# Transposes some steps later, banks' additions ahead of later remainders, and the norm's work in pieces: a two-layer hybrid encoder on one core

## The chip, the core and the metric

The kernel runs on one core of one Trainium2 chip. The metric is the device time of the core in microseconds, and the number compared is the median of several runs. The core has five engines that matter here. TensorE (PE; its weight loads are listed as PEld) multiplies. VectorE (DVE) and ScalarE (ACT) do elementwise work and read the accumulators. GpSimd (POOL) does elementwise work on the main on-chip memory and issues some transfers. SyncE (SP) issues most transfers. Each engine has its own queue of instructions and they meet only at semaphores.

## The reference

The reference is a trunk of two residual layers over 256 tokens of width 2048, in float32. Each layer adds a token mixer and then a gated feed-forward part, each of them on the RMS-normed tokens:

```
for i in range(DEPTH):                     # DEPTH = 2
    h = rms_norm(x, norm_mix[i])
    if i % 2 == 0:
        mix = attention_mixer(h, ...)      # 16 query heads, 4 key heads of 128, softmax over 256 tokens
    else:
        mix = recurrent_mixer(h, ...)      # two projections, conv of width 4, two gated scans, output projection
    x = x + mix
    x = x + swiglu(rms_norm(x, norm_ffn[i]), w_gate, w_up, w_down)   # width 5632
```

In the attention mixer, queries and keys of each head are RMS-normed and rotated before the scores. In the recurrent mixer, the x branch is convolved, goes through a forward and a backward gated linear recurrence, and is multiplied by GELU of the gate branch.

## The kernel before

**Numbers in two parts.** TensorE gets every float32 operand as two parts: a rounded part (`hi`) and a remainder (`lo`), and a product is three matmuls (hi·hi, hi·lo, lo·hi). Weights come in halves of 128 x 1024 numbers (512 KB). `load_half` loads one into `raw` (SP's queue), ScalarE casts it to `hi` (L129) and VectorE subtracts to get the remainder `lo` (L130). Each of the three tiles has 5 buffers. The list `order` holds all 704 halves in the order in which TensorE takes them, and `taken[0]` counts them.

**Who sets the order.** TensorE's order is that of the program text. The order of the other engines is laid by a planner that simulates the program and picks ready instructions by their place in it. Two things bind the planner: `follow(i, j)` puts instruction i behind j on its engine without a semaphore, and `in_line` chains the casts on ScalarE, and the remainders on VectorE, in the order of the halves. `in_line` is on only in the feed-forward parts, where `line` is filled (`line.update`) and afterwards cleared.

**A clock of steps.** `step()` counts half products of TensorE (three matmuls are two steps; in the three-matmul sums of the recurrent mixer one step). `later(delay, fn)` puts work off until the count has gone on by `delay`; one item comes at each step at most, in the order in which they were put in. So the attention's small matmuls are strewn among the projections' large ones: the keys' transposes (`KEY_TURN`, `turn_heads`, L663), the queries' (`TURN_Q`), the scores of the four heads of a group (`SCORES`, L719), the transposes of the softmax's probabilities (`TURN_P` after the scores, L737), and the sums of values (`VALUES`, L751). The keys' operand is `hq`, scaled by `scale` on VectorE (L677); the probabilities are scaled on GpSimd (L731) by the reciprocal of their sum (L729). `flush` runs what is left at the end of the attention.

**Accumulators.** The large products go into four banks of the pool `ps_a` (tag `acc`), the small ones into four of `ps_m` (tag `pm`). `project_tokens` fills two banks from 8 halves (`token_half`). `project_pair` fills four banks, for two column blocks j = 0, 1: some steps for both blocks, then the rest of block 0, then the rest of block 1. At a step in `forms` it does the two halves of a block pair in seven products instead of eight (`seven_forms`: L295 to L304 make the sums of weights that this needs; the second half comes through `sr`, which GpSimd's queue loads and adds up in flight). `merge` (L385 to L389) puts the seven products together. When block j is complete, `done(j, banks)` adds the banks to what they belong to on VectorE: gate (L819), up (L822), residual tokens `x_tok` (L565, L542). In the recurrent mixer L896 takes the gate branch's bank. Only then can the bank be filled anew.

**The norm.** `Norm.add(c)` is called when a column block of 512 of the residual is complete: squares on ScalarE, `turned` (two 32 x 32 block transposes on VectorE and 16 copies, eight of them on each of two engines, L516), and four operands (a cast, L462, and a subtraction, L463). It ran in one go. `owed` is a list of pieces of work that `project_pair` calls between halves with `settle`; before, only the transposes, copies and casts of a feed-forward unit's result (L836 to L850) go through it.

## Time and profile before

| | |
|---|---|
| median of 3 runs | 1980.67 us (1979.37 to 1981.26) |
| profiled execution | 1983.66 us |
| its span, first to last instruction | 1981.9 us |
| TensorE's mean granted clock | 0.998 |
| HBM traffic over the span | 216 GB/s |

One execution was profiled. Its time is that of the whole execution, its span that from the first to the last instruction. All stages and rows below are in microseconds from the start of the span. The profile's page gives the busy share of each engine; the list of waits says which engine waited for whom; the timeline gives start, length and, in brackets, the idle time before an instruction and what ended it. A matmul's length includes the time in the pipeline, so two matmuls in a row overlap in it. The stages of the time before lie so: keys and values from 6 to 50, queries with the attention in between from 50 to 170, the attention's output from 170 to 270, the feed-forward part of layer 0 from 270 to 968, the recurrent mixer from 968 to 1199, its output from 1199 to 1288, the feed-forward part of layer 1 from 1288 to the end.

### The profile page before, as it was taken

The page shows a single profiled execution, that of the slowest core. Times are in us where ns is not written, and L with a number is a line of the kernel's source. Part 1 is how long each engine was busy: PE and PEld are TensorE (multiplying, and loading weights), DVE is VectorE, ACT ScalarE, POOL GpSimd, SP SyncE. Part 2 cuts the span into 40 slices and gives each one's busy share as a digit, 9 for nine tenths or more (in the row PEclk, how much of TensorE's full clock was granted, in tenths as well). Part 3 has the DMA queues.
Part 4 walks back from the last instruction along what each step waited for, and adds up shares of the span by engine and source line. Part 5 has one row for each costly group of instructions (what it writes and reads, how often), then busy time and mean ns, then how long its engine had stood idle before and what let it go on. Part 6 is the DMA issues. An engine that isn't in the chain of part 4 may idle for free.

```text
span 1981.9 us, 27557 instructions
## 1 busy us (share of the span) xinstructions
PE 1962.5 (99%) x9665; PEld 1661.3 (84%) x9665; DVE 1686.6 (85%) x2273; ACT 1347.1 (68%) x2050; POOL 221.6 (11%) x317
## 2 busy tenths in 40 slices
PE   9999999999999999999999999999999999999999
PEld 7788887888888888888899998888888888888887
DVE  6676888867999988999978886998768999989998
ACT  6566667655677656677798986767746776567773
POOL 0011101000001110011033331000000101011010
PEclk9999999999999999999999999999999999999999
DMA  8544657767767876676656556567767778777784
GB/s 332 168 139 133 202 198 214 248 213 221 231 217 241 264 251 222 232 230 221 204 172 193 183 175 208 192 210 225 228 206 229 232 227 266 230 252 228 231 262 166
DMA packets 133771, 430.75 MB, mean 217 GB/s; under 512 B 14976, under 2 KB 15872, under 8 KB 133376
## 3 DMA queue, kind: packets, MB, share of 16 engines
q1 hardware_dynamic: 109008, 362.11, 53.2%
q0 software_dynamic: 24480, 66.86, 13.9%
q8 instruction: 76, 1.25, 0.3%
q14 instruction: 63, 0.52, 0.1%
q10 hardware_dynamic: 144, 0.02, 0.0%
HBM read 426.83 MB, written 2.10 MB: 216 GB/s over the span
## 4 chain that ended last, share of the span: by engine, by line
PE 83%; DVE 8%; issue 4%; ACT 4%; DMA 2%; POOL 0%; SPq 0%; DVEq 0%; ACTq 0%; POOLq 0%
PE acc L339 51%; PE acc L256 9%; PE pm L339 9%; PE acc L394 3%; PE acc L393 3%; PE acc L395 3%; DVE lo L130 3%; ACT tf L842 1%; PE pm L256 1%; ACT hi L129 1%; PE pm L394 1%; PE pm L393 1%; PE pm L395 1%; DMA raw<-in_w_gate_dram 1%; DVE lo L301 1%
## 5 line engine op out<-in xcount | busy, mean ns | idle before, releaser
L130 DVE TENSOR_TENSOR lo<-raw,hi 128x1024 fp32r<-128x1024 f32 (+1 forms) x620 | 748.9, 1225 | 168.2 <-ACT hi L129 163.6
L129 ACT CAST hi<-raw 128x1024 fp32r<-128x1024 f32 (+1 forms) x620 | 638.0, 1047 | 316.3 <-PE acc L339 171.1
L339 PE MATMUL acc<-hi,xg 128*128 128x512 f32 x1920 | 614.1, 389 | 3.3 <-DVE fg L819 3.1
L339 PE MATMUL acc<-hi,act 128*128 128x512 f32 x1370 | 434.1, 390 | 2.3 <-DVE x_tok L565 1.2
L339 PEld LDWEIGHTS acc<-hi,xg 128*128 128x128 f32 x1920 | 360.4, 188 | 79.9 <-DVE fg L819 4.0
L339 PE MATMUL acc<-lo,xg 128*128 128x512 f32 x960 | 373.5, 389 | 0.0
L339 PEld LDWEIGHTS acc<-hi,act 128*128 128x128 f32 x1370 | 257.2, 188 | 56.3 <-DVE x_tok L565 1.8
L339 PE MATMUL acc<-lo,act 128*128 128x512 f32 x685 | 266.7, 389 | 1.3 <-DVE lo L130 1.3
L339 PEld LDWEIGHTS acc<-lo,xg 128*128 128x128 f32 x960 | 180.2, 188 | 37.3
L842 ACT COPY tf<-tb 32x256 f32<-32x256 f32 x352 | 142.2, 404 | 17.3 <-DVE tb L836 13.4
L339 PEld LDWEIGHTS acc<-lo,act 128*128 128x128 f32 x685 | 128.7, 188 | 27.8 <-DVE lo L130 1.7
L394 PE MATMUL acc<-xg,hi 128*128 128x256 f32 x512 | 144.8, 283 | 0.6 <-DVE xg L463 0.6
L393 PE MATMUL acc<-xg,hi 128*128 128x256 f32 x512 | 144.9, 283 | 0.1
L395 PE MATMUL acc<-xg,lo 128*128 128x256 f32 x512 | 144.4, 282 | 0.0
L302 ACT CAST wxh<-raw 128x1024 fp32r<-128x1024 f32 x85 | 89.3, 1050 | 74.0 <-DVE raw L300 73.5
L281 POOL DMA_DIRECT2D sr<-in_w_up_dram x64 | 35.6, 557 | 775.1 <-DVE lo L301 694.0
L298 ACT CAST wxh<-wx 128x512 fp32r<-128x512 f32 x85 | 52.8, 621 | 91.6 <-DVE wx L295 58.8
L297 ACT CAST hi<-sr 128x1024 fp32r<-128x1024 f32 x85 | 89.3, 1051 | 35.2 <-PE acc L339 31.4
L304 DVE TENSOR_TENSOR wxl<-raw,wxh 128x1024 fp32r<-128x1024 f32 x85 | 103.5, 1217 | 7.6 <-ACT wxh L302 7.6
L256 PE MATMUL acc<-hi,xg 128*128 128x512 f32 x320 | 109.3, 402 | 0.4 <-ACT hi L129 0.4
L301 DVE TENSOR_TENSOR lo<-sr,hi 128x1024 fp32r<-128x1024 f32 x85 | 103.4, 1217 | 0.0
L394 PEld LDWEIGHTS acc<-xg,hi 128*128 128x128 f32 x512 | 97.9, 191 | 0.9 <-DVE xg L463 0.8
(212 smaller groups left out, 3178.4 us busy)
## 6 DMA issues: line engine op xcount, KB each, us to landing
raw<-in_w_gate_dram SPq DMA_DIRECT2D x176, 512.0 KB, 5.4
raw<-in_w_down_dram SPq DMA_DIRECT2D x155, 512.0 KB, 5.1
raw<-in_w_up_dram SPq DMA_DIRECT2D x112, 512.0 KB, 5.6
sr<-in_w_up_dram POOLq DMA_DIRECT2D x64, 512.0 KB, 4.7
raw<-in_w_in_dram SPq DMA_DIRECT2D x64, 512.0 KB, 4.5
raw<-in_w_qkv_dram SPq DMA_DIRECT2D x48, 512.0 KB, 4.3
raw<-in_w_o_dram SPq DMA_DIRECT2D x32, 512.0 KB, 3.5
wx<-in_w_up_dram SPq DMA_DIRECT2D x64, 256.0 KB, 4.6
```

The lines of the kernel that those rows point to most:

```text
L129: newest["cast"] = in_line("act", act.copy(hi[:, sl, :], raw[:, sl, :]))
L130: in_line("dve", dve.tensor_tensor(lo[:, sl, :], raw[:, sl, :], hi[:, sl, :].bitcast(F32), ALU.subtract))
L256: pe.matmul(accs[a], x, wt[:, k, :], start=(k0 + k == 0 and n == 0), stop=(end and k == 1 and n == 2))
L297: in_line("act", act.copy(hi, raw))
L301: in_line("dve", dve.tensor_tensor(lo, raw, hi[:].bitcast(F32), ALU.subtract))
L302: in_line("act", act.copy(xh[:, 1:, :], r1))
L304: in_line("dve", dve.tensor_tensor(xl[:, 1:, :], r1, xh[:, 1:, :].bitcast(F32), ALU.subtract))
L339: pe.matmul(acc, a, b, start=id(acc) not in begun, stop=last and i == 2)
L393: pe.matmul(o, hi, x[:, :S], start=start, stop=False)
L394: pe.matmul(o, hi, x[:, S:], start=False, stop=False)
L395: pe.matmul(o, lo, x[:, :S], start=False, stop=stop)
L842: n = act.copy(f[32 * i : 32 * i + 32, q::4, :, :], b[32 * q : 32 * q + 32, :, i, :, :])
```

## The change

- `KEY_TURN` goes from (36, 44) to (62, 68) steps. `TURN_P` becomes one number for each head, 16 for the first two and 20 for the others. The second entry of `VALUES` goes from 94 to 98.
- `not_after(i)` notes that instruction i has to come ahead of the remainder of the half `taken[0] + 3`; `settled`, called with each remainder, then makes this remainder follow i on VectorE. Bound like this are the additions L819, L822, L565, L542 and, for the last two column tiles, L896. `seven_forms` counts its two halves one by one for this.
- `Norm.add` no longer does its work at once but puts six pieces into `owed`: squares and block transposes, four pieces of four copies, and the operands. In the feed-forward parts the copies follow the newest cast and the newest remainder. The last column's call does all that is owed at once. `token_half` calls two pieces for each half, `project_pair` one, or two where more than six are owed; at a step for one block, all are called only where the step before was for both.
- The first weight half is loaded in two transfers and the second one is loaded and cast in two; x's tiles 2 and 3 are loaded behind the second half instead of the first.

The diff without the pure moves of `owed` and `settle`:

```diff
-KEY_TURN = (36, 44)
+KEY_TURN = (62, 68)
-TURN_P = 16
-VALUES = (62, 94)
+TURN_P = (16, 16, 20, 20)
+VALUES = (62, 98)
...
+    due = {}
+
+    def not_after(i, ahead=3):
+        due.setdefault(taken[0] + ahead, []).append(i)
+
+    def settled(i, n):
+        for k in [k for k in due if k <= n]:
+            for j in due.pop(k):
+                follow(i, j)
...
-        newest["load"] = sync.dma_start(out=raw[:, :n, :], in_=src[:, :n, :])
+        for i in range(pieces):
+            sl = slice(i * n // pieces, (i + 1) * n // pieces)
+            newest["load"] = sync.dma_start(out=raw[:, sl, :], in_=src[:, sl, :])
...
-            in_line("dve", dve.tensor_tensor(lo[:, sl, :], raw[:, sl, :], hi[:, sl, :].bitcast(F32), ALU.subtract))
+            rest = in_line("dve", dve.tensor_tensor(lo[:, sl, :], raw[:, sl, :], hi[:, sl, :].bitcast(F32), ALU.subtract))
+            settled(rest, taken[0] - 1)
...
             scale_x(0)
+            return load_half(*order[n], 2)
+        if n == 1:
             return load_half(*order[n], 2, partial(load_x, 2, 2))
...
     def token_half(accs, xs, k0):
         half()
+        settle(2)
...
-        taken[0] += 2
+        taken[0] += 1
         load_half(*order[i])
+        taken[0] += 1
...
-        in_line("dve", dve.tensor_tensor(lo, raw, hi[:].bitcast(F32), ALU.subtract))
+        settled(in_line("dve", dve.tensor_tensor(lo, raw, hi[:].bitcast(F32), ALU.subtract)), taken[0] - 1)
...
-            if len(cols) == 1:
+            if len(cols) == 1 and i and len(plan[i - 1][1]) == 2:
                 settle(-1)
                 if ready:
                     ready()
-                    ready = None
...
                 if i:
-                    settle()
+                    settle(2 if len(owed) > 6 else 1)
...
         def add(self, c):
-            for a in range(2):
-                act.activation(tmp("nj", (P, WIDE), mybir.dt.bfloat16, 1), x_tok[:, a, c, :], AF.Square, accum_out=self.sums[:, a, c : c + 1])
-            behind = self.finish() if c == NCOL - 1 else None
-            for f in turned(x_tok[:, :, c, :], True, behind):
-                self.operand(f, True)
...
+            last = c == NCOL - 1
+            parts = []
+            fields = {}
+
+            def first():
+                for a in range(2):
+                    act.activation(tmp("nj", (P, WIDE), mybir.dt.bfloat16, 1), x_tok[:, a, c, :], AF.Square, accum_out=self.sums[:, a, c : c + 1])
+                fields["behind"] = self.finish() if last else [line.get(e) for e in ("act", "dve")]
+                fields["b"] = fp[0].tile([P, 2, FOUR, P], F32, tag="tb", name=nm("tb"))
+                fields["f"] = fp[0].tile([P, 8, FOUR, 32], F32, tag="tf", name=nm("tf"))
+                for a in range(2):
+                    dve.transpose(fields["b"][:, a, :, :], x_tok[:, a, c, :])
+
+            def copies(q):
+                b, f = fields["b"], fields["f"]
+                behind = fields["behind"] if last else [line.get(e) for e in ("act", "dve")]
+                for i in range(4):
+                    o, y = f[32 * i : 32 * i + 32, q::4, :, :], b[32 * q : 32 * q + 32, :, i, :]
+                    n = (dve.tensor_copy if i % 2 else act.copy)(o, y.rearrange("p a (k t) -> p a k t", k=FOUR))
+                    if behind and behind[i % 2] is not None:
+                        follow(n, behind[i % 2])
+
+            def operands():
+                for k in range(FOUR):
+                    self.operand(fields["f"][:, :, k, :], True)
...
+            owed.extend([first, *(partial(copies, q) for q in range(4)), operands])
+            if last:
+                settle(-1)
...
-                dve.tensor_tensor(y, y, acc, ALU.add)
+                not_after(dve.tensor_tensor(y, y, acc, ALU.add))
...
-            later(TURN_P, turn)
+            later(TURN_P[h], turn)
...
-                        dve.tensor_tensor(g[:, a, :], acc, g[:, a, :], ALU.add)
+                        not_after(dve.tensor_tensor(g[:, a, :], acc, g[:, a, :], ALU.add))
...
-                        dve.tensor_tensor(u[:, a, :], acc, u[:, a, :], ALU.add)
+                        not_after(dve.tensor_tensor(u[:, a, :], acc, u[:, a, :], ALU.add))
...
-        dve.tensor_tensor(y, acc, nr.r, ALU.mult)
+        i = dve.tensor_tensor(y, acc, nr.r, ALU.mult)
+        if ct >= KT - 2:
+            not_after(i)
```

More of the change, by code (lines that the diff above doesn't have):

```diff
@@ L272, in square, with settle @@
         return t.rearrange("p c f -> p (c f)")
+    owed = []
+    def settle(n=1):
+        while owed and n:
+            owed.pop(0)()
+            n -= 1
     coming, ahead = [], []
@@ L319, in x_forms @@
         return [(t[:, 0, i, :], t[:, 1, i, :]) for i in range(4)]
-    owed = []
-    def settle(n=1):
-        while owed and n:
-            owed.pop(0)()
-            n -= 1
     def project_pair(xs, forms, plan, middle, done, ready=None):
@@ L468, in add @@
         def add(self, c):
-            for a in range(2):
-                act.activation(tmp("nj", (P, WIDE), mybir.dt.bfloat16, 1), x_tok[:, a, c, :], AF.Square, accum_out=self.sums[:, a, c : c + 1])
-            behind = self.finish() if c == NCOL - 1 else None
-            for f in turned(x_tok[:, :, c, :], True, behind):
-                self.operand(f, True)
-            for n in THREE[1:] if self.seven else ():
-                if FOUR * c <= 2 * n < FOUR * c + FOUR:
-                    self.forms[n] = x_forms(self.xs[2 * n], self.xs[2 * n + 1], f"nf{n}")
+            last = c == NCOL - 1
[20 more added lines that the diff above has]
+                    self.operand(fields["f"][:, :, k, :], True)
+                for n in THREE[1:] if self.seven else ():
+                    if FOUR * c <= 2 * n < FOUR * c + FOUR:
+                        self.forms[n] = x_forms(self.xs[2 * n], self.xs[2 * n + 1], f"nf{n}")
+            owed.extend([first, *(partial(copies, q) for q in range(4)), operands])
+            if last:
+                settle(-1)
         def finish(self):
@@ L502, in spread @@
             return i
-    def turned(src, both=True, behind=None):
-        b = fp[0].tile([P, 2, FOUR, P], F32, tag="tb", name=nm("tb"))
-        f = fp[0].tile([P, 8, FOUR, 32], F32, tag="tf", name=nm("tf"))
-        for a in range(2):
-            dve.transpose(b[:, a, :, :], src[:, a, :])
-        for q in range(4):
-            for i in range(4):
-                o, y = f[32 * i : 32 * i + 32, q::4, :, :], b[32 * q : 32 * q + 32, :, i, :]
-                y = y.rearrange("p a (k t) -> p a k t", k=FOUR)
-                turn = dve.tensor_copy if i % 2 and both else act.copy
-                n = turn(o, y)
-                if behind is not None:
-                    follow(n, behind[i % 2])
-        return [f[:, :, k, :] for k in range(FOUR)]
     fp = []
```

2 lines of the change are left out of this document (1 added, 1 removed).

## The prediction

> **What bounds the kernel now.** I read the page first, then the list of waits, then the timeline of each engine around every place where TensorE stood still. The share of busy time comes from the page, the other lines from the list of waits (engine, line, whom it waited for: us in total, times, longest):
> ```profile
> PE 1962.5 (99%) x9665; PEld 1661.3 (84%) x9665; DVE 1686.6 (85%) x2273; ACT 1347.1 (68%) x2050; POOL 221.6 (11%) x317
> ```
> ```profile
> PE acc L339 <- DVE fg L819: 3.1, 2, 2.4
> ...
> PE pm L663 <- DVE hq L677: 3.0, 1, 3.0
> ...
> PE pm L737 <- POOL pr L731: 1.9, 3, 0.6
> ...
> PE acc L339 <- DVE lo L130: 1.3, 1, 1.3
> PE acc L339 <- DVE x_tok L565: 1.2, 1, 1.2
> ...
> PE acc L339 <- DVE gl L896: 1.1, 1, 1.1
> ...
> PE pm L256 <- DVE lo L130: 0.8, 1, 0.8
> ```
> TensorE is the bound: 1962.5 of 1981.9 us. No edit here removes a matmul, so all that can be won are those waits and what hangs on them. They are few and each has one place. What else can matter is how far VectorE runs ahead, so here are stretches of the trace (busy us and count of PE, weight load, DVE, ACT, POOL, then the granted clock, DMA share, GB/s); the last is a whole unit of the feed-forward part:
> ```profile
> 60.00:64.00 4.00, 1.00 (x5) 0.54 (x3) 3.90 (x9) 0.70 (x2) 0.00 (x0) 0.89 0.56 155
> ...
> 66.00:68.00 2.00, 2.00 (x6) 1.61 (x5) 0.69 (x1) 0.06 (x1) 0.00 (x0) 0.50 0.01 4
> ...
> 823.70:865.50 41.80, 41.80 (x183) 34.23 (x183) 39.54 (x51) 30.22 (x44) 4.25 (x6) 1.00 0.75 239
> ```
> The unit gives 183 matmuls in 41.80 us: one starts every 0.228 us, though one takes 0.39. So an idle stretch costs its length, plus 0.39 - 0.23 = 0.16, plus 0.11 because the matmul behind it takes 0.50: **idle + 0.27 us**. And VectorE is busy 39.54 of 41.80 us there: it has next to no time to spare.
>
> **Part 1, keys' transposes (36, 44 to 62, 68 steps).**
> ```profile
> 60.45 0.39 PE L256 MATMUL acc<-hi,xg 128*128 128x512 f32 x1
> 63.84 1.50 PE L663 MATMUL pm<-ident,hq 128*128 128x128 f32 x4 [3.00 <-DVE hq L677]
> ...
> 70.14 0.60 PE L663 MATMUL pm<-ident,hq 128*128 128x128 f32 x4
> ...
> 63.10 1.29 DVE L677 TENSOR_TENSOR hq<-hq,hf 128x512 f32<-128x512 f32 x2
> ```
> From 60.45 to 70.14 are 9.69 us; in them lie 13 matmuls (2.96 at 0.228) and four transposes (0.4). The other 6.3 are lost: 3.2 of waiting, 0.9 of transposes that come one by one (1.50 for four instead of 0.60), and 2.3 because the clock row shows 0.50 afterwards. A step is half a product of three matmuls, 0.34 us, so 26 steps move the transposes 8.9 us back, to about 69.7; their operand is there at 64.4. The second pair moves 24 steps, behind the first. Nothing needs the keys before the first scores, which come at step 222 of the count against 188. The same eight transposes, four casts and subtractions remain, so only their place changes. I take **-6.3** (bounds: -3.9, if the slow clock struck for another reason, to -6.4).
> [...]
>
> **Part 2, probabilities' transposes of heads 2 and 3 (16 to 20 steps).**
> ```profile
> 117.37 1.00 PE L737 MATMUL pm<-ident,pr 128*128 128x128 f32 x4 [0.64 <-POOL pr L731]
> ...
> 116.83 0.93 POOL L731 TENSOR_SCALAR pr<-pr,rs 128x256 f32<-128x256 f32 x2 [5.51 <-DVE rs L729]
> ```
> Three groups have this wait, all at head 3, whose scores collide with the next group's squares and rotation: 1.9 idle in the list, and three times 0.16 + (1.00 - 0.60), 3.5 in all. Four steps are 1.36 us against 1.2 of lateness, so it just suffices. **-3.3** (-1.2 to -3.5). The weighted sum of values moves from 94 to 98 with it; in the last group the flush at step 96 catches it, 8 steps (2.7 us) ahead of its use, which covers one cast and one subtraction.
>
> **Part 3, banks' additions bound ahead of the remainder three halves later.** The order on VectorE is what is edited: no instruction is added.
> ```profile
> 314.14 1.22 DVE L301 TENSOR_TENSOR lo<-sr,hi 128x1024 fp32r<-128x1024 f32 x1
> ...
> 315.88 0.68 DVE L819 TENSOR_TENSOR fg<-acc,fg 128x512 f32<-128x512 f32 x1
> ...
> 316.61 0.50 PE L339 MATMUL acc<-hi,xg 128*128 128x512 f32 x1 [2.42 <-DVE fg L819]
> ...
> 1332.04 0.50 PE L339 MATMUL acc<-hi,xg 128*128 128x512 f32 x1 [0.70 <-DVE fg L819]
> ...
> 1376.77 0.50 PE L339 MATMUL acc<-hi,xg 128*128 128x512 f32 x1 [0.22 <-DVE fu L822]
> ...
> 1204.55 0.50 PE L339 MATMUL acc<-hi,act 128*128 128x512 f32 x1 [1.06 <-DVE gl L896]
> ...
> 924.01 0.50 PE L339 MATMUL acc<-hi,act 128*128 128x512 f32 x1 [1.22 <-DVE x_tok L565]
> ```
> A new unit needs the banks of the last; their additions stood behind remainders not needed for another 5 us (L301 ahead of L819). Bound, they run as soon as the bank is closed. At 316.61, 1332.04 and 1376.77 this frees 2.7 + 1.0 + 0.5 = 4.2 us. But VectorE's work is not less, and its remainders for the next units come no sooner:
> ```profile
> 333.08 2.35 DVE L130 TENSOR_TENSOR lo<-raw,hi 128x1024 fp32r<-128x1024 f32 x2
> ...
> 336.01 0.39 PE L339 MATMUL acc<-lo,xg 128*128 128x512 f32 x1
> ...
> 375.74 2.35 DVE L130 TENSOR_TENSOR lo<-raw,hi 128x1024 fp32r<-128x1024 f32 x2
> ...
> 377.80 0.39 PE L339 MATMUL acc<-lo,xg 128*128 128x512 f32 x1
> ...
> 330.98 0.69 DVE L303 TENSOR_TENSOR wxl<-wx,wxh 128x512 fp32r<-128x512 f32 x1 [3.05 <-ACT wxh L298]
> ```
> The remainder used at 336.01 is done at 333.08 + 1.2 = 334.3, 1.7 us ahead; one unit later (377.80) it is 0.9 ahead. If TensorE comes 2.7 us sooner and VectorE doesn't, the wait returns there and only 0.9 stays. VectorE's own 3.05 idle in between (it waits behind ScalarE's 16 copies, which start after the additions) can shrink, so up to all can stay. I take 1.1 and 0.9 for the two layers, **-2.0** (-0.9 to -4.2). At 1204.55 nothing of the kind follows (the list has a single wait of this stage's products on a remainder, that of part 4): **-1.3** (0 to -1.3). At 924.01 it is 1.5, counted in part 4.
> What the binding costs: where VectorE runs ahead it now waits for the bank.
> ```profile
> 499.68 1.28 DVE L819 TENSOR_TENSOR fg<-acc,fg 128x512 f32<-128x512 f32 x2
> 501.26 1.22 DVE L130 TENSOR_TENSOR lo<-raw,hi 128x1024 fp32r<-128x1024 f32 x1 [0.30 <-ACT hi L129]
> ```
> Here a remainder of 1.2 us ran just before the pair; now the pair goes first, waits some 0.5 for its bank, and the line behind it (remainder, sums of the next seven-product step) is that much later. In the units that follow, VectorE is full (39.54 of 41.80), so what the lead doesn't take comes out as a wait of TensorE: in four such runs of units (two in each layer) about half of the 0.5, **+0.9** (0 to +3).
>
> **Part 4, norm's work in pieces.**
> ```profile
> 939.79 2.38 DVE L516 COPY tf<-tb 32x256 f32<-32x256 f32 x8
> 942.21 3.50 DVE L130 TENSOR_TENSOR lo<-raw,hi 128x1024 fp32r<-128x1024 f32 x3
> ...
> 943.48 0.50 PE L339 MATMUL acc<-lo,act 128*128 128x512 f32 x1 [1.28 <-DVE lo L130]
> ...
> 908.00:966.00 58.00, 55.50 (x244) 45.32 (x243) 53.83 (x80) 42.95 (x76) 6.07 (x4) 1.00 0.68 226
> ```
> Eight copies stood ahead of the remainder that TensorE waited for: 1.55 lost. Now a piece (four copies, two on each of two engines) comes with each half, and behind that half's cast and remainder. A half is 2.7 us of TensorE against 1.2 of remainder, so a piece of about 0.6 fits. With the 1.5 at 924.01: **-2.6** of 3.0 (0 to -3.0), as VectorE has only 58.0 - 53.8 = 4.2 us free in that stage. The last column's work still comes in one go at the end, as before; it costs what it did. In the two output projections the pieces have remainders far ahead as cover; were it gone, each piece could cost its 0.6.
>
> **Part 5, the first loads.**
> ```profile
> 8.09 1.05 ACT L129 CAST hi<-raw 128x1024 fp32r<-128x1024 f32 x1 [1.75 <-DMA raw<-in_w_qkv_dram]
> ...
> 10.45 0.50 PE L256 MATMUL pm<-lo,xg 128*128 128x512 f32 x1 [0.76 <-DVE lo L130]
> ...
> 0.00:15.00 15.00, 12.60 (x53) 10.40 (x54) 7.24 (x11) 9.12 (x14) 0.41 (x5) 1.00 0.89 330
> ```
> The second half now goes ahead of 256 KB of x, and it and the first come as two transfers each, cast as they land. 256 KB at the 330 GB/s of the first 15 us take 0.8 us; the first piece gains that twice, so it is cast at some 6.5 instead of 8.09 and its remainder is there before 9.5. 0.76 + 0.27 go. The two more issues on SP's queue push x's second part and the third half back by under 1 us, ahead of casts that wait for ScalarE anyhow. **-1.1** (0 to -1.8).
>
> **The sum**: -6.3 - 3.3 - 2.0 - 1.3 + 0.9 - 2.6 - 1.1 = -15.7 us. The profiled execution took 1983.66 us with a span of 1981.9; it would take 1968.0. The median of the three runs is 1980.67 (1979.37 to 1981.26), 3 us below it, so **1965.0**.
>
> **The rivals.**
> *All waits go and nothing is handed back* (0.18): 6.3 + 3.5 + 4.2 + 1.3 + 3.0 + 1.1 = 19.4, 1961. VectorE's 3.05 idle speaks for it, its 39.54 of 41.80 against.
> *Half of it* (0.22): ScalarE's, VectorE's and SP's orders are not written out but laid by the planner, so an edit at one place can reorder others; head 3 or the pieces then still wait, or the binding fixes an order that stood already, and parts 1, 5 and half of the rest stay: about -10, 1971.
> *Slower, by the binding* (0.05): VectorE reaches the bound remainder early at most of the 22 units and stands still. Each time it loses what is left of the bank, up to half a half, about 1.2 us; 22 of them are 26 against 16.6 won: 1990. It decides from the point where VectorE arrives over 0.7 us ahead of the bank's end in nearly every unit. Against it: between units it mostly has merges and sums of its own to do, and in the full unit the pair already runs late.
> [...]
> *Nothing to measure* (0.05): the clock's part or the units give back what the rest wins, 1977 to 1984.
>
> **How the numbers follow.** The forecast, 1965.0 with its own 1961.5 to 1968.5, has 0.5. The range takes in the next two: from 1959 (all bounds at their best give 1960.5, and the runs lie up to 1.3 below their median) to 1973. A measurement of this kernel tells about 0.2%, 4 us, from no change: faster 0.9, same 0.05, slower 0.05.
>
> **What would show it.** Right: no idle of TensorE and no 0.50 clock between 60 and 70; transposes of four in 0.60 near 117; no wait on L819, L822, L565, L896; new waits of under 1.2 us on a remainder in units 1 and 2; none at 943. Wrong: the keys still waiting, a wait that recurs in every unit on L130 or L301, or ScalarE's copies ahead of casts.

## The result and the profile after

The changed kernel takes 1965.91 us (median of 6 runs, 1964.75 to 1967.08); the kernel before, run beside it, 1980.97 us (6 runs, 1979.37 to 1983.44). The ratio is 0.9923 with a 95% interval of 0.9911 to 0.9936: faster by 12.7 to 17.6 us. The profiled execution took 1964.75 us with a span of 1963.0. So the two profiled spans are 18.9 us apart and the medians 15.1; why these differ is told below.

The page's busy times and the whole list of TensorE's waits after the change (in the list: us in total, times, longest):

```profile
PE 1954.5 (100%) x9665; PEld 1660.3 (85%) x9665; DVE 1686.6 (86%) x2274; ACT 1344.2 (68%) x2051; POOL 222.3 (11%) x317
```
```profile
PE pm L536 <- DVE ndg L530: 1.6, 1, 1.6
PE acc L409 <- ACT xg L478: 1.1, 1, 1.1
PE pm L458 <- POOL ones L455: 1.0, 1, 1.0
PE acc L272 <- ACT hi L141: 0.5, 1, 0.5
PE acc L356 <- DVE gl L920: 0.2, 1, 0.2
PE acc L272 <- DVE lo L142: 0.2, 1, 0.2
```

None of the waits on the keys, the probabilities, the gate's, up's and residual's additions is left. (Lines have moved: L819 is now L843, L822 L846, L565 L589, L896 L920, L130 L142, L663 L687, L737 L761.) TensorE does the same 9665 matmuls, and DVE's busy time is the same 1686.6 us. But two waits stand at the head of the list that the kernel before did not have in this form: for the norm's scaled identity `ndg` (L530) and for an operand `xg` (L478).

The timeline of TensorE shows the small transposes, each four of them in 0.60 us with no wait in brackets:

```profile
68.59 0.60 PE L687 MATMUL pm<-ident,hq 128*128 128x128 f32 x4
...
107.08 0.60 PE L761 MATMUL pm<-ident,pr 128*128 128x128 f32 x4
```

Since TensorE's order hardly changes, the same matmul, counted from the first one, can be looked up in both traces. The difference of its starts is what has been won by then (us from the start of each span):

| matmul | before | after | won so far | won since the row above, and where |
|---|---|---|---|---|
| 51 | 14.44 | 13.50 | 0.94 | 0.94, first loads |
| 481 | 111.79 | 104.58 | 7.21 | 6.27, keys |
| 901 | 190.63 | 179.80 | 10.83 | 3.62, probabilities |
| 1501 | 324.00 | 310.31 | 13.69 | 2.86, first unit to second |
| 1701 | 369.64 | 355.65 | 13.99 | 0.30, second to third |
| 4101 | 914.69 | 899.65 | 15.05 | 1.06, the other units of layer 0 |
| 4251 | 951.80 | 933.65 | 18.15 | 3.10, the two waits at 924 and 943 |
| 4451 | 984.68 | 968.90 | 15.77 | **-2.38, the end of layer 0's norm** |
| 6301 | 1213.09 | 1196.47 | 16.62 | 0.85, the gate branch's bank at 1204 |
| 7051 | 1384.65 | 1366.47 | 18.18 | 1.56, first units of layer 1 |
| 9665 | 1977.81 | 1958.98 | 18.83 | 0.65, the other units of layer 1 |

Each trace is one execution, so a row can hold what belongs to that execution and not to the kernel; where the other traces show that, it is said below. Two things are not what I forecast. Nothing is handed back in the units; and 2.4 us are handed back at a place that I had called unchanged. Here are that place's lines on VectorE and TensorE, after the change:

```profile
949.94 0.69 DVE L589 TENSOR_TENSOR x_tok<-x_tok,acc 128x512 f32<-128x512 f32 x1
950.55 1.22 DVE L142 TENSOR_TENSOR lo<-raw,hi 128x1024 fp32r<-128x1024 f32 x1
951.68 0.71 DVE L496 STREAM_TRANSPOSE tb<-x_tok 128x512 f32<-128x512 f32 x1
952.31 1.19 DVE L142 TENSOR_TENSOR lo<-raw,hi 128x1024 fp32r<-128x1024 f32 x1
953.41 0.15 DVE L520 TENSOR_REDUCE nrt<-nsq 128x2 f32<-128x8 f32 x1
953.77 1.22 DVE L142 TENSOR_TENSOR lo<-raw,hi 128x1024 fp32r<-128x1024 f32 x1 [0.20 <-ACT hi L141]
954.92 0.16 DVE L521 TENSOR_SCALAR nrt<-nrt 128x2 f32<-128x2 f32 x1
956.65 1.23 DVE L142 TENSOR_TENSOR lo<-raw,hi 128x1024 fp32r<-128x1024 f32 x1 [1.58 <-ACT hi L141]
957.80 0.15 DVE L556 TENSOR_TENSOR rsq_s<-nrt,nr 128x2 f32<-128x2 f32 x1
...
958.37 0.48 DVE L530 TENSOR_SCALAR ndg<-ident,nr 128x128 f32<-128x128 f32 x2
```
```profile
958.72 0.71 PE L536 MATMUL pm<-ndg,ones 128*128 128x128 f32 x4 [1.62 <-DVE ndg L530]
...
961.92 0.38 PE L409 MATMUL acc<-xg,hi 128*128 128x256 f32 x1 [1.07 <-ACT xg L478]
```

The chain from the last bank's addition (L589) to the scaled identity (L530) has four weight remainders (L142) between its links. The last of them stands 1.58 us idle for its cast, which itself waits for TensorE to free a `hi` buffer; the link behind it (L556) starts at 957.80, though its operand `nr` is done at 956.72. From L589 to the end of L530 are 950.63 to 958.85, 8.2 us. In the kernel before they were 5.3 (the second L565 ended at 968.88, L491 at 974.13), with two remainders in between:

```profile
967.60 1.28 DVE L565 TENSOR_TENSOR x_tok<-x_tok,acc 128x512 f32<-128x512 f32 x2
...
970.02 1.18 DVE L130 TENSOR_TENSOR lo<-raw,hi 128x1024 fp32r<-128x1024 f32 x1
971.12 0.15 DVE L481 TENSOR_REDUCE nrt<-nsq 128x2 f32<-128x8 f32 x1
971.31 0.17 DVE L482 TENSOR_SCALAR nrt<-nrt 128x2 f32<-128x2 f32 x1
971.92 1.23 DVE L130 TENSOR_TENSOR lo<-raw,hi 128x1024 fp32r<-128x1024 f32 x1 [0.45 <-ACT hi L129]
973.07 0.15 DVE L532 TENSOR_TENSOR rsq_s<-nrt,nr 128x2 f32<-128x2 f32 x1
...
973.65 0.48 DVE L491 TENSOR_SCALAR ndg<-ident,nr 128x128 f32<-128x128 f32 x2
```

### The profile page after: what moved, and what is told of

Its sections match the earlier page's. It is cut to its first block, busy times and chain, and to the rows that moved or that the text cites. A ratio compares the mean times of both kernels' runs of the same rounds, so it can differ in the third digit from the quotient of the medians.

```text
span 1963.0 us, 27585 instructions
## 1 busy us (share of the span) xinstructions
PE 1954.5 (100%) x9665; PEld 1660.3 (85%) x9665; DVE 1686.6 (86%) x2274; ACT 1344.2 (68%) x2051; POOL 222.3 (11%) x317
## 4 chain that ended last, share of the span: by engine, by line
PE 98%; ACT 1%; DVE 1%; issue 0%; DMA 0%; DVEq 0%; ACTq 0%
PE acc L356 63%; PE pm L356 12%; PE acc L272 10%; PE acc L410 3%; PE acc L409 3%; PE acc L411 3%; PE pm L272 1%; PE pm L410 1%; PE pm L409 1%; PE pm L411 1%; PE pm L743 1%; PE pm L775 1%; PE pm L761 0%; ACT sg L607 0%; ACT L607 0%
## 5 line engine op out<-in xcount | busy, mean ns | idle before, releaser
L142 DVE TENSOR_TENSOR lo<-raw,hi 128x1024 fp32r<-128x1024 f32 (+1 forms) x621 | 748.4, 1229 | 130.6 <-ACT hi L141 127.7
```

What stands on the lines that cost most here:

```text
L142: rest = in_line("dve", dve.tensor_tensor(lo[:, sl, :], raw[:, sl, :], hi[:, sl, :].bitcast(F32), ALU.subtract))
```

## The experiments

Twelve kernels in three groups of four, each timed in five rounds beside the kernel before, whose medians in the three groups were 1981.04, 1979.87 and 1980.51 us. A gain is worked out from the ratio to the kernel before in the same group, so it can differ by some tenths from the difference of medians. Line numbers in an experiment's rows are its own. "Alone" means that the kernel before was given that part only.

### The parts alone

**Keys alone:**

```diff
-KEY_TURN = (36, 44)
+KEY_TURN = (62, 68)
```

> Before with the keys' transposes alone moved (62, 68). Theory: the wait of 3.0 us, the transposes that come one by one and the slow clock are one thing, so all go: 6.3 us faster (about 1974.7), no idle of TensorE and a clock of 1.00 between 60 and 70 us. Rival: the slow clock had another cause and stays: 3.9 us faster (about 1977). Second rival: the transposes find another thing late at their new place: under 3 us faster.

Measured: 1974.82 us, ratio 0.9971 (0.9961 to 0.9981), so 5.7 us less (3.8 to 7.7), as the theory had it. There is no wait on the keys and no slow clock.

**Probabilities alone:**

```diff
-TURN_P = 16
-VALUES = (62, 94)
+TURN_P = (16, 16, 20, 20)
+VALUES = (62, 98)
...
-            later(TURN_P, turn)
+            later(TURN_P[h], turn)
```

> Before with the probabilities' transposes of heads 2 and 3 alone moved by 4 steps (and the second sum of values from 94 to 98). Theory: 1.36 us of shift covers 1.16 of lateness in three groups: 3.3 to 3.5 us faster (about 1977.5), transposes of four in 0.60 us. Rival: GpSimd's scaling comes as much later as the order on ScalarE moves: at most 1.2 us faster.

Measured: 1977.22 us, ratio 0.9982 (0.9973 to 0.9991), 3.6 us less (1.8 to 5.3). The gain is as the theory had it, and the three waits on GpSimd are gone. This profile holds a surprise besides: the key wait is there in full, with no slow clock behind it. Here are TensorE's row of that wait and the window behind it (columns as in the prediction's table of windows), and then the same window of the kernel before:

```profile
63.70 0.33 PE L663 MATMUL pm<-ident,hq 128*128 128x128 f32 x1 [3.00 <-DVE hq L677]
...
64.50:70.00 5.50, 5.50 (x29) 4.56 (x28) 2.61 (x3) 2.77 (x4) 0.00 (x0) 1.00 0.20 63
```
```profile
64.50:70.00 5.50, 5.50 (x15) 4.44 (x16) 1.67 (x2) 1.63 (x2) 0.00 (x0) 0.50 0.16 64
```

The idle time is 3.00 us in both, and the granted clock is 1.00 in one and 0.50 in the other, with 29 matmuls in the window against 15.

**Binding alone:** `due`, `not_after` and `settled` with all their calls, as in the change; nothing of the norm's pieces. Its core:

```diff
-                        dve.tensor_tensor(y, y, accs[a][:, sl], ALU.add)
+                        not_after(dve.tensor_tensor(y, y, accs[a][:, sl], ALU.add))
...
-                        dve.tensor_tensor(g[:, a, :], acc, g[:, a, :], ALU.add)
+                        not_after(dve.tensor_tensor(g[:, a, :], acc, g[:, a, :], ALU.add))
```

> Before with the bound additions alone. Theory now: with the additions early, a unit's product, its block transposes and ScalarE's 16 copies start earlier, VectorE waits less behind them, and nothing is handed back: in the two layers' units 0 to 2 4.4 us go, at the recurrent mixer's end 0.8, the small waits on remainders of units 6, 9 and 10 about 1.2; the 1.5 at 924 come back at 943, where VectorE is late. About 6.4 us faster (1974.6); VectorE's wait for ScalarE's cast in unit 1 falls from 3.05 to about 1.5 us. Rival, as forecast: the waits return at remainders in units 1 and 2 (0.9 stays in each layer) and the binding costs 0.9: about 2 us faster (1979), with waits of TensorE on remainders there.

Measured: 1975.07 us, ratio 0.9973 (0.9961 to 0.9984), 5.3 us less (3.2 to 7.7). All waits on L819, L822 and L565 are gone, and no wait came back at a remainder in the units, so the rival falls. The median is near the theory's 1974.6. One part of the theory missed: the 1.5 us at 924 did not come back at 943, and the wait on a remainder there, which the pieces were to cure, is gone too. And the two new waits are there:

```profile
PE pm L509 <- DVE ndg L503: 1.6, 1, 1.6
PE acc L405 <- ACT xg L474: 1.1, 1, 1.1
```

**The norm's pieces alone:** `Norm.add` and the calls of `settle` as in the change, nothing bound. Its core:

```diff
-            for f in turned(x_tok[:, :, c, :], True, behind):
-                self.operand(f, True)
...
+            owed.extend([first, *(partial(copies, q) for q in range(4)), operands])
+            if last:
+                settle(-1)
```

> Before with the norm's pieces alone. Theory: the wait at 943 (1.55) goes; the wait at 924 on a bank's addition stays or shrinks; and the new waits at the end of layer 0's norm (1.9 on the scaled identity, 1.8 instead of 1.3 on the last operands) come from the pieces, since the last column's work now comes after the casts in the planner's order: the sum is about 0 (1980 to 1982). Rival: those new waits come from the binding of the last column's additions, or only from the earlier start of everything: then 1.5 to 3 us faster.

Measured: 1979.84 us, ratio 0.9997 (0.9987 to 1.0006): no difference that can be told. I had thought that the pieces made the new waits. They did not: no wait on `ndg` appears in this list, only 0.6 on `xg` as before. The theory of the waits fell, and the rival, that the binding makes them, holds; its 1.5 to 3 us did not come, though. The two waits at 924 and 943 are not gone:

```profile
PE acc L352 <- DVE x_tok L585: 1.0, 2, 0.8
...
PE acc L406 <- DVE xg L475: 0.6, 1, 0.6
...
PE acc L352 <- DVE lo L140: 0.3, 1, 0.3
```

TensorE's idle time is 0.81 us at the first and 0.33 at the second. The four other traces with neither binding nor pieces (keys, probabilities, first loads, six steps) have 0.72 to 1.09 and 0.43 to 1.16 there; that the pieces shorten these waits is not shown.

**First loads alone:**

```diff
-        newest["load"] = sync.dma_start(out=raw[:, :n, :], in_=src[:, :n, :])
+        for i in range(pieces):
+            sl = slice(i * n // pieces, (i + 1) * n // pieces)
+            newest["load"] = sync.dma_start(out=raw[:, sl, :], in_=src[:, sl, :])
...
+            return load_half(*order[n], 2)
+        if n == 1:
             return load_half(*order[n], 2, partial(load_x, 2, 2))
```

> The kernel before, with the first key half's load and the token tiles' loads alone as in the change (the half goes out in two pieces, the second pair of token columns is loaded a half later). My theory: the first wide product starts about 1.1 us earlier and nothing is given back, so 1.0 to 1.2 us less than before (about 1979.9, ratio 0.9994); all of the other waits of before stay. Rival: the pieces only move the start, and the second and third half arrive no earlier, so that TensorE waits for them instead: 0 to 0.3 us less, with new idle time between 8 and 16 us.

Measured: 1981.62 us, ratio 1.0007 (0.9998 to 1.0015): no gain, where I expected 1.0 to 1.2 us. Its 51st matmul does start 0.76 us earlier (13.68 against 14.44). But then:

```profile
63.73 1.29 DVE L681 TENSOR_TENSOR hq<-hq,hf 128x512 f32<-128x512 f32 x2
...
64.47 0.33 PE L667 MATMUL pm<-ident,hq 128*128 128x128 f32 x1 [4.39 <-DVE hq L681]
```

TensorE comes earlier and stands 4.39 us instead of 3.00 for keys that come 0.63 us later (L677 started at 63.10 before), because VectorE's work on them fell into another order. An earlier start was worth nothing here, ahead of a wait whose end did not move with it. My rival was of the same kind but at another place (the second and third half), so neither text named it.

### Taken out of the change again

**The change without the pieces:** binding, keys, probabilities and first loads; `Norm.add` as before.

> The changed kernel without the norm's work in pieces: keys, probabilities, binding and first loads as in the change, the norm's squares, transposes, copies and operands issued at once as before. My theory: with the additions bound, the bank waits at 924 and 943 us are gone already (they were, with the binding alone), so the pieces are worth nothing here: 1965.5 to 1967 us, the same as the changed kernel, and the wait for the scaled identity (1.8 us) and for the last column's operands (1.2 + 0.4 us) at the end of layer 0's norm stand in the profile. Rival, that the pieces do carry their part of the gain as I forecast: 1968 to 1969 us, with waits of about 1.3 us near 908 and 925 us.

Measured: 1965.70 us (1965.15 to 1966.33), ratio 0.9929 (0.9916 to 0.9941): the same as the changed kernel. With the binding there, the pieces are worth nothing; there is no wait at 908 or 925, and both new waits stand.

**The change without the first loads** (the diff of the first loads undone).

> The changed kernel with the first loads as before (the first key half's load in one piece, the token tiles in their old order). Alone, the first loads gave nothing: TensorE started the wide products 0.5 to 0.9 us earlier and then waited that much longer for the keys, which came no earlier. My theory: in the changed kernel the key wait is gone, so there the earlier start is kept, and without it the time is 0.8 to 1.2 us longer, 1966.7 to 1967.1 us. Rival: the start is not worth anything in either kernel, 1965.7 to 1966.2 us.

Measured: 1966.67 us (1966.1 to 1967.62), ratio 0.9930 (0.9918 to 0.9943). That is 0.8 us more than the changed kernel, with intervals that overlap; the times alone can't tell. The traces help: over the seven profiles with the new loads the 51st matmul starts at 13.44 to 13.94, over the others at 13.98 to 14.46 (one at 15.23, where wide matmuls lay 0.43 instead of 0.23 us apart from 7.5 to 10). So about 0.6 us by the means of the two groups without that one. The key wait swallowed it in the run with the first loads alone; with the key wait gone, nothing in the list of waits takes it back.

### The new waits at the norm's end

**Stage later**, in the changed kernel:

```diff
-NORM = 20
+NORM = 26
```

> The changed kernel with the norm's spreading stage due 26 steps after its bank instead of 20, in both attention norms' places where it is used. My theory: the late thing is the chain of the norm itself, which stands behind four weight remainders on VectorE; the last column's operands come at 961.8 us whatever the stage does, so the 1.9 us wait for the scaled identity only joins the wait for them: 1965.0 to 1967 us, no difference from the changed kernel, with one idle stretch of about 3 us in place of two. Rival, that the stage is merely due too early: the 1.9 us go and nothing takes their place, 1964.0 us or less (a difference from the changed kernel of -1.9 us).

Measured: 1967.91 us (1966.16 to 1968.83), ratio 0.9938 (0.9924 to 0.9951). The two waits became one, as expected, but the time is above my 1965 to 1967. The row of the list of waits, then the windows behind the wait here and in the changed kernel:

```profile
PE acc L409 <- ACT xg L478: 3.4, 1, 3.4
```
```profile
963.00:967.00 4.00, 3.65 (x16) 3.42 (x17) 1.68 (x4) 1.77 (x5) 0.20 (x4) 0.57 0.04 14
```
```profile
963.00:967.00 4.00, 4.00 (x35) 4.00 (x35) 2.87 (x6) 2.76 (x5) 0.20 (x4) 1.00 0.02 4
```

The chain does not care for the step: counted from the start of the 4251st matmul, the wait for the operands ends after 28.26 us here and after 28.27 in the changed kernel. And one wait of 3.4 us had a half clock behind it (0.57 is the mean of a window that holds some full clock too), which the two waits of 1.6 and 1.1 had not. So a later due step is no cure: TensorE loses 1.5 us more here than in the changed kernel (by the starts of matmuls 4376 and 4551 in both).

**The last column's additions not bound**, all others bound, in the changed kernel:

```diff
-                        not_after(dve.tensor_tensor(y, y, accs[a][:, sl], ALU.add))
+                        (not_after if norm is None or c + j < NCOL - 1 else id)(dve.tensor_tensor(y, y, accs[a][:, sl], ALU.add))
```

> The changed kernel with all additions bound but those of the last column at the end of layer 0's last down bank. My theory: the new waits for the scaled identity and the last operands come from just this binding: with these two additions first, four remainders fall between the links of the norm's chain instead of two. Without it the chain from the bank's end to the scaled identity takes about 6 us instead of 9, the wait for the scaled identity (1.78 + 0.1 us) goes, that for the operands is 0.3 to 1.3 us as in the kernel before, and the time is 1.8 to 2.5 us under the changed kernel, 1963.4 to 1964.1 us. Rival: the pile of remainders there comes from the additions of the banks ahead of it; the two waits stay, 1965.5 to 1966.5 us.

Measured: 1963.02 us (1962.7 to 1964.4), ratio 0.9913 (0.9900 to 0.9927). The wait for the scaled identity is gone, and the one on `xg` is that of the kernel before, 0.6 in the list. On VectorE a remainder is again ahead of the two additions, two are left in the chain, and the scaled identity is done at 956.4 instead of 958.85:

```profile
948.75 1.23 DVE L142 TENSOR_TENSOR lo<-raw,hi 128x1024 fp32r<-128x1024 f32 x1 [1.45 <-ACT hi L141]
949.89 1.28 DVE L589 TENSOR_TENSOR x_tok<-x_tok,acc 128x512 f32<-128x512 f32 x2
...
955.93 0.48 DVE L530 TENSOR_SCALAR ndg<-ident,nr 128x128 f32<-128x128 f32 x2
```

So just this binding made the two waits: the time from the end of the second addition to the end of the scaled identity is 5.2 us here, against 5.3 in the kernel before. With the binding the additions are first by one remainder, and the chain behind them is last by two.

**The chain bound too**, in the changed kernel: the last operand's subtraction (L479) has to come ahead of the remainder five counts on, and so the whole chain before it.

```diff
-            dve.scalar_tensor_tensor(lo, x, g, hi.bitcast(F32), ALU.mult, ALU.subtract)
+            newest["xlo"] = dve.scalar_tensor_tensor(lo, x, g, hi.bitcast(F32), ALU.mult, ALU.subtract)
...
-                    self.operand(fields["f"][:, :, k, :], True)
+                    self.operand(fields["f"][:, :, k, :], True), (last and not self.seven and k == FOUR - 1) and not_after(newest["xlo"], 5)
```

> The changed kernel with one more binding: the remainder of the last column's last operand at the end of layer 0's last down bank is put ahead of the weight remainder five halves on, so that the chain of the norm (mean, scaled identity, copies, operands) no longer stands behind the remainders of the halves four and five ahead. My theory: both new waits go (1.78 + 0.1 us for the scaled identity, 1.23 + 0.4 + 0.1 us for the operands) and the halves put back have lead enough (9 us and more, of which about 6 are used): 3.3 to 3.7 us less than the changed kernel, 1962.2 to 1962.6 us, ratio to before 0.9904 to 0.9908. Rival: the wait moves on to the halves put back, a wait for lo of 1 to 3 us between 961 and 966 us, and the time stays at 1965 to 1966 us.

Measured: 1962.84 us (1962.21 to 1966.5), ratio 0.9918 (0.9904 to 0.9931), 2.9 us less than the kernel without the pieces in the same group (1965.70). VectorE's rows:

```profile
953.71 0.17 DVE L521 TENSOR_SCALAR nrt<-nrt 128x2 f32<-128x2 f32 x1
954.38 0.16 DVE L556 TENSOR_TENSOR rsq_s<-nrt,nr 128x2 f32<-128x2 f32 x1 [0.50 <-ACT nr L607]
...
954.97 0.48 DVE L530 TENSOR_SCALAR ndg<-ident,nr 128x128 f32<-128x128 f32 x2
```

The wait on `ndg` is gone, that on `xg` fell to 0.3 in the list, and no remainder is late. I had 3.3 to 3.7 us; 0.4 of the rest is still with `xg`, because on ScalarE a weight cast ran ahead of the operands, and 0.4 came back 13 us later, where TensorE now waits for `xs` (L439).

**The same on ScalarE:** in addition, the four scaled operands (L478) are bound ahead of the weight cast six counts on.

```diff
+    casts = {}
...
-            newest["cast"] = in_line("act", act.copy(hi[:, sl, :], raw[:, sl, :]))
+            newest["cast"] = in_line("act", act.copy(hi[:, sl, :], raw[:, sl, :])); [follow(newest["cast"], j) for j in casts.pop(taken[0] - 1, [])]
...
-            i = act.activation(hi, x, AF.Copy, scale=g)
+            newest["xhi"] = i = act.activation(hi, x, AF.Copy, scale=g)
...
-                    self.operand(fields["f"][:, :, k, :], True), (last and not self.seven and k == FOUR - 1) and not_after(newest["xlo"], 5)
+                    self.operand(fields["f"][:, :, k, :], True), (last and not self.seven and k == FOUR - 1) and (not_after(newest["xlo"], 5), casts.setdefault(taken[0] + 6, []).append(newest["xhi"]))
```

> The version of the run before (last column's operands bound ahead of the weight remainder five halves on) with one more order: on ScalarE the last column's four scaled operands are put ahead of the weight cast six halves on. In the run before that cast stood between the copies and the operands (957.57 to 958.52 us), and TensorE waited 0.42 + 0.4 + 0.1 us for the first operands. My theory: the operands come 1 us earlier, these 0.9 us go, nothing else waits: 1961.7 to 1962.2 us. Rival: the later cast delays a remainder that TensorE needs, or the operands' remainders on VectorE are the late ones: 1962.5 to 1963.5 us.

Measured: 1962.49 us (1962.05 to 1962.68), ratio 0.9908 (0.9895 to 0.9922), the best of all: 18.2 us under the kernel before. I had 1961.7 to 1962.2. The wait on `xg` is gone from the list; the 0.4 for `xs` stay. The step from the version above is 0.35 us by the medians, within their scatter.

### The key wait, a little later

**Six steps**, in the kernel before:

```diff
-KEY_TURN = (36, 44)
+KEY_TURN = (42, 50)
```

> The kernel before with the keys' transposes at steps 42 and 50 in place of 36 and 44 (the change has 62 and 68). Six steps of about 0.45 us are 2.7 us, so of the 3.2 us wait 0.5 to 1.2 us are left. My theory: the half-clock stretch comes with an idle time of 3 us and more, not with the transposes themselves, so that a wait of about 1 us costs itself alone: all matmuls behind it 227 ns apart, and the time 4.0 to 5.5 us under before (1974.5 to 1976), against 6.2 with the wait quite gone. Rival: the clock falls after any wait of a microsecond with small transposes behind it: 200-ns excesses on 5 to 12 matmuls as in before, and 2 to 3.5 us under before.

Measured: 1980.22 us, ratio 0.9998 (0.9989 to 1.0007): nothing. Both expectations missed, since the wait is not 0.5 to 1.2 us but as long as ever. VectorE's rows, then TensorE's with the window behind it:

```profile
62.52 0.17 DVE L532 TENSOR_TENSOR rsq_s<-hv,hf 128x8 f32<-128x8 f32 x1
63.34 1.23 DVE L130 TENSOR_TENSOR lo<-raw,hi 128x1024 fp32r<-128x1024 f32 x1 [0.65 <-ACT hi L129]
64.48 0.16 DVE L533 SCALAR_TENSOR_TENSOR rsq_s<-rsq_s,hf 128x8 f32<-128x8 f32 x1
64.67 0.17 DVE L534 SCALAR_TENSOR_TENSOR hf<-rsq_s,hf 128x8 f32<-128x8 f32 x1
64.88 1.29 DVE L677 TENSOR_TENSOR hq<-hq,hf 128x512 f32<-128x512 f32 x2
```
```profile
65.62 0.33 PE L663 MATMUL pm<-ident,hq 128*128 128x128 f32 x1 [2.72 <-DVE hq L677]
...
66.00:70.00 4.00, 3.77 (x13) 3.05 (x14) 0.86 (x2) 0.59 (x1) 0.00 (x0) 0.65 0.33 122
```

TensorE stands still 2 us later than before, so by then it has freed one more `hi` buffer. The next cast (at 62.26, behind a wait for TensorE) and its remainder run, and the remainder lands between L532 and L533 of the keys' own chain; `hq` (L677) starts at 64.88 instead of 63.10. The six steps are eaten by one remainder. With the change's 26 steps the same remainder enters the chain (in the run with the keys alone `hq` starts at 64.70 and is done at 66.0), but the transposes come only at 69.37, so the chain ends first. It is the mechanism of the norm's end once more. The theory on the clock missed too: half clock came behind 2.72 us of idle already (last section).

## Why the prediction was right, and where it was not

The forecast was 1965.0 us (1959.0 to 1973.0), the result 1965.91. The cause forecast, that TensorE is the bound and that the waits named go, is right: the parts alone (5.7 for the keys, 3.6 for the probabilities, 5.3 for the binding) and 0.6 for the first loads (from the traces) come to 15.2 us, each gain known to about 2 us, and the medians are 15.1 apart. That the forecast came within a microsecond was luck: several terms were off, to both sides, and an error in the subtraction made up for the rest.

- **Keys, -6.3:** 6.27 in the two traces, 5.7 (3.8 to 7.7) alone. Right. Two things in its working were not. The operand was not there at 64.4 but at 66.0 (keys alone), since a remainder entered its chain; the 26 steps covered that. And the 2.3 us of slow clock are not a fixed price: in the run with the probabilities alone the same 3.00 us of idle had none behind it, and in the kernel before the half clock lasted 6.82 us, twice as long as in any other run (last section).
- **Probabilities, -3.3:** 3.62 and 3.6 (1.8 to 5.3). Right.
- **Units, -2.0:** 2.86 + 0.30 + 1.56 = 4.7 in the traces. The step that failed is "If TensorE comes 2.7 us sooner and VectorE doesn't, the wait returns there". VectorE did come sooner. Its row for that remainder in the second unit and the gap ahead of it:

```profile
317.43 0.69 DVE L327 TENSOR_TENSOR wxl<-wx,wxh 128x512 fp32r<-128x512 f32 x1 [1.50 <-ACT wxh L322]
...
319.53 2.35 DVE L142 TENSOR_TENSOR lo<-raw,hi 128x1024 fp32r<-128x1024 f32 x2
```

  The remainder starts at 319.53 instead of 333.08, 13.55 us earlier; ahead of the units everything was 10.83 earlier. VectorE thus gained 2.7 us, as much as TensorE. The 3.05 us idle ahead of L303 (now L327) is 1.50 in all eight traces with the binding and 3.05 in all six without it. Over the whole kernel VectorE's wait there falls from 45.9 to 39.3 us, with the binding alone as in the changed kernel. By the order in the traces, additions that come early let ScalarE's 16 copies, and so the cast that VectorE waits for, come early; this path was not tested by itself. The prediction had nothing handed back as the upper bound of the step.

  But not all of the 4.7 us is the binding's. In the profiled execution of the kernel before, the cast ahead of the first unit's end waited for a weight transfer:

```profile
307.12 1.05 ACT L129 CAST hi<-raw 128x1024 fp32r<-128x1024 f32 x1 [2.06 <-DMA raw<-in_w_gate_dram]
```

  In the other thirteen traces the same cast waited 0.2 to 0.7 us, and in the five of them without the binding TensorE stood 0.70 to 0.87 us for L819 there, instead of 2.42. Behind the remainder of this cast VectorE has no idle time up to L819, so all of it came later: 1.6 to 1.7 us of the 2.42 that the prediction put down to the order on VectorE were this transfer. Against those five traces VectorE gains 0.9 to 1.0 us at the remainder above, TensorE 1.0 to 1.2 by the second unit, and the three stretches together 2.8 to 3.6 us: nearer to the 2.0, and still with nothing handed back.
- **Cost of the binding, +0.9:** 1.06 + 0.65 were gained in these rows, so no cost shows. The 1.06 in layer 0 are not the binding's gain, though. Of the other traces without the binding three lose nothing there against the changed kernel (0.02 at most), and of those with it two lose 0.7 (binding alone, stage later). Five of the fourteen traces lose 0.7 to 1.3 us there, and in just these a cast waited 3.7 to 4.2 us for a weight transfer (in the kernel before at 789.01); in the others no such wait there is over 3.5. In layer 1's other units the binding does help: 592.5 to 592.9 us in all traces with it, 592.9 to 594.5 in those without.
- **The gate branch's bank at 1204, -1.3:** 0.85. What is left (0.23 idle) is no remainder that the binding could pass.
- **Norm in pieces, -2.6:** the waits at 924 and 943 went, 3.10 in the traces, but the cause was wrong. The binding alone takes both away; the pieces alone gave 0.6 (from 2.6 less to 1.2 more), and beside the binding nothing. The forecast credited them with the gain of another part.
- **"The last column's work still comes in one go at the end, as before; it costs what it did":** this failed, by 2.38 us. The work is the same, but the binding moved remainders between its links. The run with that one binding undone gave 2.35 us back in the trace.
- **First loads, -1.1:** the right sign and too large, about 0.6 over the profiles, and nothing at all while the key wait stood.

In the traces the misses that made me too low, 2.7 for the units, 2.6 for the binding's cost and about 0.8 in parts 2 and 4, come to 6.1; those on the other side, 2.4 for the norm's end, 0.45 at 1204 and 0.16 for the loads, to 3.0. So the two profiled spans should differ by 15.7 + 3.1 = 18.8, and they do, by 18.9.

The medians differ by 3.8 less. The profiled run after lies 1.2 below its median, and that of before 2.7 above its own (1983.66 against 1980.97); where such an excess sits, the other profiles tell. From the start of the 251st matmul to that of the 301st (the key wait and the slow clock) it took 16.75 us, and 14.19, 15.67 and 15.57 in the runs of probabilities, binding and pieces alone, which have the same key steps. (The first loads alone have them too and took 17.17, with the longer wait of 4.39.) From the 1451st to the 1501st (the first unit's end) it took 14.19 us, and 12.33 to 12.50 in the five others without a binding. So 1.1 to 2.6 and 1.7 to 1.9 us of what I summed were that execution's own, and the 1.06 us in layer 0 came with a late transfer as well; in layer 1's other units it was quicker than four of those five. I knew that it was 3 us above the median, and still subtracted the whole sum from the median; that error and the 3.1 us by which the sum was too small nearly cancelled.

What stays open: whether the 0.4 us for `xs` and the 0.5 us for the gate branch's bank can be had too, which was not tried, and why a weight transfer lands late in one execution and not in another.

## What to carry to other kernels

Where one engine serves, in an order laid beforehand, both a stream (here: weights' remainders, each of which waits in the end for TensorE) and short chains that go back and forth between engines, bind whole chains and not single links: at the norm's end an early first link only let the stream into the gaps behind it, and in the run with six steps a consumer moved back let in more of it. Price each part with the others there, since one wait can swallow the gain of an earlier edit (first loads) and one edit can take another's gain (binding and pieces). And before a sum is subtracted from a median, set the largest terms against a second execution, and look what the wait itself waited for: the largest one in the units stood behind a late transfer.

## What the hardware showed unexpectedly

The half clock behind an idle stretch of TensorE comes or stays away from one execution to the next: behind 3.00 us of idle it was 0.50 for 5.5 us in one and 1.00 in another; behind 1.6 us it stayed at 1.00. Executions of one and the same kernel differ as well: over the eleven runs with the six steps the mean granted clock was 0.998 to 1.000.

The traces record when the granted clock changes. Here is the half clock in the kernel before and in the run with the pieces alone (columns as above):

```profile
63.16:69.98 6.82, 6.01 (x16) 4.66 (x17) 2.88 (x4) 1.63 (x2) 0.00 (x0) 0.50 0.24 78
```
```profile
63.92:67.33 3.41, 3.13 (x10) 2.56 (x10) 1.00 (x2) 0.59 (x1) 0.00 (x0) 0.50 0.33 130
```

It lasts 3.41 us or, in the kernel before, twice that. These are the key waits of the runs that have one, and what came behind them:

| run | idle of the key wait | its length | half clock |
|---|---|---|---|
| before | 60.84 to 63.84 | 3.00 | from 63.16, 6.8 us |
| probabilities alone | 60.69 to 63.70 | 3.00 | none |
| binding alone | 61.63 to 64.63 | 3.00 | from 65.06, 3.4 us |
| pieces alone | 60.68 to 63.69 | 3.00 | from 63.92, 3.4 us |
| first loads alone | 60.08 to 64.47 | 4.39 | from 65.29, 3.4 us |
| six steps | 62.90 to 65.62 | 2.72 | from 67.23, 3.4 us |

The length of the wait alone does not tell what follows: behind the same 3.00 us came no half clock, 3.4 us of it and 6.8 us of it, and behind 4.39 us no more than 3.4. The wait of 3.4 us at the norm's end in the run with the stage later had one behind it too (0.57 from 963 to 967). Behind the changed kernel's 1.62 and 1.07 at the norm's end the clock stayed at 1.00, and so it did behind the 2.42 at the first unit of the kernel before (1.00 from 316 to 322). What decides between these was not shown. In the kernel before the clock fell at 63.16, ahead of the first transpose at 63.84, so the transposes did not bring that fall. Whether they kept it down longer was not tested. The price of one such stop is thus its idle time and, at the key wait of these runs, a half clock of 0, 3.4 or 6.8 us.
